# A split store, a new order of rotary units and pinned merge loads in a one-layer hybrid step

## The chip, the cores and the metric

The kernel runs on one core of a Trainium2 chip. The core has a matrix engine (TensorE, PE in the profile, with its weight loads shown as PEld), three engines for elementwise work (VectorE or DVE, ScalarE or ACT, GpSimd or POOL), and SyncE (SP), which here issues the transfers. The engines run their own instruction lists in order and meet by semaphores. The metric is the device time of one execution in microseconds. Each run comes with the granted clock of TensorE as a share of its full speed.

## The reference, cut to what matters

One layer of a hybrid backbone for 128 context and 1024 latent tokens, model width 1024. Both token groups go through the same weights, so the kernel carries them as one set of T = 1152 columns.

```python
def trunk_layer(x, mod, cache, lb, norm_g, ffn1, ffn2, mixer_w):
    m = [mod[:, i][:, None, :] for i in range(N_MOD)]
    x = x + 0.5 * m[2] * swiglu(modulate(x, norm_g[0], m[0], m[1]), *ffn1)
    mix, ctx = token_mixer(modulate(x, norm_g[1], m[3], m[4]), cache, lb, *mixer_w)
    x = x + m[5] * mix
    x = x + 0.5 * m[8] * swiglu(modulate(x, norm_g[2], m[6], m[7]), *ffn2)
    return x, ctx

# in token_mixer: attention of 8 heads and a two-way recurrent scan on the same input
    o_rec = rmsnorm(o_fw + flip(o_bw), hg_norm_g) * jax.nn.silu(heads(hgate, HG_DV))
    merged = jax.nn.sigmoid(ga) * (o_attn @ w_up_attn) + jax.nn.sigmoid(gr) * (o_rec @ w_up_rec)
    out = merged @ w_out
```

The keys of the attention have a rotary part that all heads share; its rotation depends on the position of a latent token on a grid. The results are the normalised x of both groups, the context's compressed keys, its rotary keys and its scan states.

## The kernel before

All values are float32. A product of two matrices is made of three matmuls: each operand is split into a high part, rounded by a cast to a shorter format, and a low part, the rest, and `mm3` (lines 516 to 518) adds high by high, high by low and low by high. So each operand costs a cast (as a rule on ScalarE) and a subtraction (on VectorE or GpSimd) before it can be used.

The stages follow one another on the columns: first feed-forward block, mixer, merge, second feed-forward block. In the mixer the recurrent part runs first. For each pair p of its heads, `proj_gate` ends with a gate: for each of three chunks of 384 columns, `put` multiplies the normalised scan output by the gate on GpSimd and stores the product, in full, in the DRAM tensor `orec`.

`attn` then makes the compressed keys, the rotary keys and the compressed queries. Units of 384 columns are run in a fixed list: k0, k1, k2 are the units of the compressed key (each has three steps: project and square, normalise, write) and r0, r1, r2 those of the rotary key (line 1276 on; a projection of 24 matmuls, then copies and products on VectorE that write tile `krt`). From the fifth step on, one step of `rec_half` is taken with each: it loads a quarter of the recurrent output, casts it on ScalarE and subtracts on VectorE (lines 1313 and 1314), since `rec_sums` computes the recurrent half of the merge's products for the two middle quarters of the columns in advance, and stores them in `ahead`.

`heads` runs eight heads, each in two blocks of 512 queries (`block`): scores against 9 key tiles, an exponential on ScalarE, its cast there (line 1512), its subtraction (line 1514) on VectorE or GpSimd, and the product with the values (`av`, lines 1481 to 1483), in which a block's output is divided by its sum (lines 1490 to 1493). In heads 6 and 7 a generator `preload` is stepped beside the blocks: it fetches what the merge will read, in chunks of 384 columns, and splits it (lines 1344 to 1346): four tiles of recurrent output, then three of attention output of heads 0 to 5. The last two heads' output is split as it comes, by `put_oat` (lines 1357 and 1358).

`merge` loads the eight x tiles and then runs `up(m)` for m = 0 to 7: the way-up weight of m is loaded, its attention half split on the chip (`raw`, `wh`, `wl`), and for each of four quarters of 288 columns the attention and the recurrent product (12 matmuls in each; the middle quarters take the recurrent one from `ahead` as tile `mu`) are multiplied by the gates `g` from `sgates`, added (tile `mt`) and split. That is 72 matmuls for each m. After m = 3, 5 and 7 a down-projection adds into x (line 545).

Tile framework and scheduler set the order: within an engine's list, instructions are placed by the scheduler's estimates unless they are pinned in program order. Transfers go out from SyncE's list one after another; a transfer that waits holds those behind it, and each one also waits until the one eight places before it has landed. Tiles of one tag share a number of buffers, so that a load waits for the last reader of an earlier tile.

Of the kernel before, what the change touches and what calls it, by code (L numbers as in the profile page):

```python
# [3 lines left out]

# [89 lines left out]
class Trunk:  # L94
# [594 lines left out]
    def mixer(self):  # L689
        nc, tc = self.nc, self.tc  # L690
        dram = lambda n, sh: self.dp.tile(sh, F32, name=n)
        self.sg = dram("sgates", [2, KT, P, T])
        self.orec = dram("orec", [4, P, T])
# [74 lines left out]
    def proj_gate(self, i, p, pair):  # L768
        nc = self.nc
        oT = pair["o"]  # L770
        assert pair["no"] == 4
        w = self.load_w(self.a["w_in"][i], KT, P, home="low")
        sq = self.tt(F32, "osq")[:, :T]
        nc.scalar.activation(sq, oT[:, :T], AF.Square)
        held, normed = [], []

        def norm():
            self.lnexp()
            for b in ORDER:
                self.rec_norm(b, oT, sq)  # L780
            normed.append(1)
            for f in held:
                f()

        def put(cs, s):
            nc.gpsimd.tensor_mul(s, oT[:, cs], s)
            nc.sync.dma_start(self.orec[p][:, cs], s)

        self.later.append(norm)
        for c in ORDER:  # L790
            ps = yield from self.proj_g(w, c)
            s = self.sigm(ps)
            nc.vector.tensor_mul(s, ps, s)  # L793
# [309 lines left out]
    def attn(self):  # L1103
# [10 lines left out]
        with tc.tile_pool(name="np", bufs=1, reuse_waits="tile") as self.fp:  # L1114
# [60 lines left out]
    def heads(self, qn, ck, ckc, KT_, ktc, rope, w0, sums):  # L1175
# [39 lines left out]
        for h in range(H):  # L1215
# [86 lines left out]
    def rec_half(self):  # L1302
# [3 lines left out]
        for k in range(4):  # L1306
            t = self.tt(F32R, "rec")
            self.rec.append((t[:, :n], t[:, n : 2 * n]))
            for v in range(2):
                c = ts(v, QW)  # L1310
# [25 lines left out]
    def preload(self):  # L1336
        nc = self.nc
        for k in (4, 5, 6, 7, 0, 1, 2):
            th, tl = self.mo[k] = self.tt(F32R, "oh"), self.tt(F32R, "ol")
            src = self.oat[k] if k < 4 else self.orec[k - 4]  # L1340
            for c in range(NCH):
                cs = slice(c * CW, (c + 1) * CW)
                raw = self.fp.tile([P, CW], F32, tag="vt", bufs=2, name="oraw")
                nc.sync.dma_start(raw, src[:, cs])
                (nc.vector.tensor_copy if k < 3 else nc.scalar.copy)(th[:, cs], raw)
                nc.vector.tensor_sub(tl[:, cs], raw, th[:, cs])
                yield

    def put_oat(self, h, r, cs, ob):
        nc = self.nc  # L1350
# [4 lines left out]
            self.mo[3] = self.tt(F32R, "oh"), self.tt(F32R, "ol")  # L1355
        th, tl = self.mo[3]
        nc.scalar.copy(th[r, cs], ob)
        nc.gpsimd.tensor_sub(tl[r, cs], ob, th[r, cs])

    def load_kv(self, src):  # L1360
        raw = self.wp.tile([P, 2, P], F32, tag="raw", bufs=2, name="raw")
# [193 lines left out]
    def merge(self):  # L1555
# [1 line left out]
        hl = self.mo  # L1557
        self.chunks, self.ticks = QORDER, 0
        self.x = []
        for k in range(KT):  # L1560
            t = self.tt(F32, f"x{k}")
            nc.sync.dma_start(t[:, :T], self.xs[k])
            self.x.append(t)

        def up(m):
            mh, ml = self.wide("mh", F32R), self.wide("ml", F32R)
            wh, wl = [self.wp.tile([P, KT, P], F32R, tag=t, bufs=3, name=t) for t in ("wh", "wl")]
            raw = self.wp.tile([P, 4, P], F32, tag="raw", bufs=2, name="raw")
            nc.sync.dma_start(raw, a["w_up"][m][:, :4])
            for i, w in enumerate((wh, wl)):  # L1570
                src = self.wrec[m // 2, i][:, 512 * (m % 2) : 512 * (m % 2) + 512]
                nc.sync.dma_start(w[:, 4:8].rearrange("p k m -> p (k m)").bitcast(F32), src)
            nc.scalar.copy(wh[:, :4], raw)
            nc.gpsimd.tensor_sub(wl[:, :4], raw, wh[:, :4])
            for c in QORDER:
                cs = slice(*c)
                mt = []
                for i in (1, 0):
                    g = self.slim("g")
                    nc.sync.dma_start(g, self.sg[i, m][:, cs])  # L1580
                    if i and REC[0] <= c[0] < REC[1]:
                        ps = self.fp.tile([P, QW], F32, tag="mu", bufs=4, name="mu")
                        nc.sync.dma_start(ps, self.ahead[m][:, c[0] - REC[0] : c[1] - REC[0]])
# [4 lines left out]
                    nc.vector.tensor_mul(t, ps, g)  # L1588
                    mt.append(t)
                nc.vector.tensor_add(mt[0], mt[1], mt[0])  # L1590
                nc.scalar.copy(mh[:, cs], mt[0])
# [751 lines left out]
```

## Time and profile before

| | |
|---|---|
| median of three runs | 2868.01 us (2866.91 to 2868.95) |
| the profiled execution | 2867.53 us, of which the span shown is 2865.3 us |
| granted TensorE clock over the span | 0.991 |
| TensorE busy | 2775.9 us, 97% |
| VectorE, ScalarE, GpSimd busy | 71%, 47%, 34% |
| rotary keys in the trace | about 1450 to 1470 us |
| heads 6 and 7 in the trace | about 1797 to 1878 us |
| merge in the trace | from 1878 us |

Rows of waits name the waiting engine, tile and line, then the engine, tile and line that released it, the total, the number of times and the longest wait. Rows of groups name line, engine, operation, written and read tiles, shapes and count, then busy time, mean ns of one, and the idle time before them with what ended it. A timeline row begins with the start and the duration. "128x288" is partitions by elements.

### The profile page before, as it was taken

The page shows a single profiled execution, that of the slowest core. Times are in us where ns is not written, and L with a number is a line of the kernel's source. Part 1 is how long each engine was busy: PE and PEld are TensorE (multiplying, and loading weights), DVE is VectorE, ACT ScalarE, POOL GpSimd, SP SyncE. Part 2 cuts the span into 40 slices and gives each one's busy share as a digit, 9 for nine tenths or more (in the row PEclk, how much of TensorE's full clock was granted, in tenths as well). Part 3 has the DMA queues.
Part 4 walks back from the last instruction along what each step waited for, and adds up shares of the span by engine and source line. Part 5 has one row for each costly group of instructions (what it writes and reads, how often), then busy time and mean ns, then how long its engine had stood idle before and what let it go on. Part 6 is the DMA issues. An engine that isn't in the chain of part 4 may idle for free. (4 is left out here: it accounts for less than half of the span.)

```text
span 2865.3 us, 55876 instructions
## 1 busy us (share of the span) xinstructions
PE 2775.9 (97%) x21222; PEld 2643.3 (92%) x21222; DVE 2029.3 (71%) x4439; ACT 1334.4 (47%) x2740; POOL 964.1 (34%) x1003
## 2 busy tenths in 40 slices
PE   8999999999999999999999999989989999999998
PEld 7999999999989999888998877789989999999997
DVE  7877777577678787876356677855765666558885
ACT  6522332321176677766535777731642322236332
POOL 0123232444222222222144444532442443424450
PEclk9999999999999999999999999999999999999999
DMA  6743443753122111112512001263543443447631
GB/s 260 228 133 119 126 127 111 250 178 118 58 70 68 43 60 38 55 46 68 181 43 77 16 16 30 82 215 99 177 154 115 144 156 119 129 143 213 202 101 67
DMA packets 218940, 331.76 MB, mean 116 GB/s; under 512 B 24048, under 2 KB 142768, under 8 KB 218672
## 3 DMA queue, kind: packets, MB, share of 16 engines
q1 hardware_dynamic: 218672, 328.20, 35.4%
q8 instruction: 167, 2.74, 0.4%
q14 instruction: 101, 0.83, 0.1%
HBM read 244.93 MB, written 83.18 MB: 115 GB/s over the span
## 5 line engine op out<-in xcount | busy, mean ns | idle before, releaser
L1802 PE MATMUL b<-xo,wo 128*128 128x288 f32 x3552 | 483.8, 295 | 1.1 <-DVE wo L1777 1.1
L1802 PEld LDWEIGHTS b<-xo,wo 128*128 128x128 f32 x3552 | 475.7, 188 | 1.3 <-DVE wo L1777 1.3
L1802 PE MATMUL b<-bh,wo 128*128 128x288 f32 x1776 | 368.0, 296 | 2.2 <-ACT et L1812 2.2
L516 PE MATMUL mm<-xh,wh 128*128 128x384 f32 x984 | 346.9, 353 | 14.1 <-DVE sg L793 5.8
L518 PE MATMUL mm<-xh,wl 128*128 128x384 f32 x984 | 335.0, 341 | 0.0
L517 PE MATMUL mm<-xl,wh 128*128 128x384 f32 x984 | 334.0, 339 | 0.0
L1802 PEld LDWEIGHTS b<-bh,wo 128*128 128x128 f32 x1776 | 290.4, 189 | 2.7 <-ACT et L1812 2.4
L545 DVE SCALAR_TENSOR_TENSOR x<-dn,modt,x 128x256 f32<-128x256 f32 (+4 forms) x472 | 225.5, 499 | 85.6 <-PE dn L518 83.7
L1802 PE MATMUL b<-bl,wo 128*128 128x288 f32 x888 | 262.5, 296 | 0.0
L1776 ACT CAST wo<-raw 128x512 fp32r<-128x512 f32 x185 | 114.7, 621 | 201.5 <-issue 85.7
L516 PEld LDWEIGHTS mm<-xh,wh 128*128 128x128 f32 x984 | 187.2, 190 | 23.0 <-DVE sg L793 7.7
L517 PEld LDWEIGHTS mm<-xl,wh 128*128 128x128 f32 x984 | 187.8, 191 | 1.1 <-issue 0.3
L2002 PE MATMUL d<-xd,wd 128*128 128x288 f32 x1344 | 179.9, 295 | 7.5 <-DVE x L1989 5.5
L518 PEld LDWEIGHTS mm<-xh,wl 128*128 128x128 f32 x984 | 187.1, 190 | 0.0
L2002 PEld LDWEIGHTS d<-xd,wd 128*128 128x128 f32 x1344 | 178.5, 188 | 8.9 <-DVE x L1989 2.7
L1777 DVE TENSOR_TENSOR wo<-raw,wo 128x512 fp32r<-128x512 f32 x185 | 127.4, 690 | 69.3 <-ACT wo L1776 66.7
L388 DVE SCALAR_TENSOR_TENSOR junk<-wada,cb 128x512 bf16<-128x512 f32 x224 | 162.1, 723 | 11.8 <-DMA wada<-in_w_aT 10.8
L1514 POOL TENSOR_TENSOR ehl<-e,ehl 128x512 fp32r<-128x512 f32 x93 | 122.1, 1318 | 140.4 <-ACT ehl L1512 73.6
L1802 PEld LDWEIGHTS b<-bl,wo 128*128 128x128 f32 x888 | 167.9, 189 | 0.0
L349 POOL TENSOR_TENSOR wl<-raw,wh 128x1024 fp32r<-128x1024 f32 (+2 forms) x48 | 95.7, 1995 | 161.2 <-ACT wh L348 121.0
L1777 DVE TENSOR_TENSOR wo<-ws,wo 128x512 fp32r<-128x512 f32 x74 | 71.4, 964 | 104.1 <-ACT wo L1776 103.6
L1776 ACT CAST wo<-ws 128x512 fp32r<-128x512 f32 x74 | 45.6, 618 | 211.9 <-POOL ws L1772 211.8
(456 smaller groups left out, 7223.1 us busy)
## 6 DMA issues: line engine op xcount, KB each, us to landing
raw<-in_w SPq DMA_DIRECT2D x148, 256.0 KB, 3.5
wada<-in_w_aT SPq DMA_DIRECT2D x112, 256.0 KB, 3.0
raw<-in_w SPq DMA_DIRECT2D x42, 512.0 KB, 3.9
raw<-in_w_in SPq DMA_DIRECT2D x41, 512.0 KB, 3.5
xr<-xd SPq DMA_DIRECT2D x56, 288.0 KB, 3.9
hr<-hs SPq DMA_DIRECT2D x26, 576.0 KB, 5.6
hb<-hd SPq DMA_DIRECT2D x44, 288.0 KB, 3.7
hs<-et SPq DMA_DIRECT2D x84, 144.0 KB, 2.2
```

Of the source, the lines that this page charges most:

```text
L349: pin((eng or self.nc.gpsimd).tensor_sub(wl, raw, wh))
L388: nc.vector.scalar_tensor_tensor(junk, ws[n % 2], 1.0, cs[s], ALU.mult, ALU.mult, accum_out=o)
L516: pin(nc.tensor.matmul(ps, wh, xh, start=start and i == 0, stop=False))
L517: pin(nc.tensor.matmul(ps, wh, xl, start=False, stop=False))
L518: pin(nc.tensor.matmul(ps, wl, xh, start=False, stop=stop and i == n - 1))
L545: nc.vector.scalar_tensor_tensor(self.x[m][:, a:b], ps[:, a - lo : b - lo], self.modt[:, gm, m, s : s + 1], self.x[m][:, a:b], ALU.mult, A ...
L1514: eng.tensor_sub(el, e, eh)
L1776: nc.scalar.copy(wh, src[i])
L1777: nc.vector.tensor_sub(wl, src[i], wh)
L1802: nc.tensor.matmul(ps, w[:, k], x[:, k, :QW], start=first, stop=last, skip_group_check=home != i)
L2002: nc.tensor.matmul(ps, w[:, k], xv, start=start, stop=stop, skip_group_check=home != i)
```

## The change

The recurrent output is stored split: `put` casts the product on ScalarE, subtracts on GpSimd, and stores the two parts with two transfers. Its readers, `rec_half` and `preload`, load both parts and compute nothing; `preload` loads them as whole tiles. The rotary units are spread over the list of units. For the last chunk of the compressed queries the subtraction is on VectorE. `preload` is stepped in all four blocks of heads 6 and 7, the cast and the subtraction of a chunk are two steps, and at its end it loads and splits the way-up weight of m = 0. The subtraction in `put_oat` goes to VectorE. In the merge the first m takes its quarters in the order 0, 3, 1, 2; the two gates of a part come in one transfer, four parts ahead, with `mu`; the x tiles are loaded two with each part; all these loads and those of the way-up weights are pinned in program order.

```diff
         def put(cs, s):
             nc.gpsimd.tensor_mul(s, oT[:, cs], s)
-            nc.sync.dma_start(self.orec[p][:, cs], s)
+            hi = self.fp.tile([P, CW], F32R, tag="t", bufs=3, name="ohi")
+            nc.scalar.copy(hi, s)
+            lo = s.bitcast(F32R)
+            nc.gpsimd.tensor_sub(lo, s, hi)
+            for v, t in enumerate((hi, lo)):
+                nc.sync.dma_start(self.orec[p, v][:, cs], t.bitcast(F32))
...
-                nc.gpsimd.tensor_sub(qn[i][1][:, cs], t, qn[i][0][:, cs])
+                eng = nc.vector if c == ORDER[-1] else nc.gpsimd
+                eng.tensor_sub(qn[i][1][:, cs], t, qn[i][0][:, cs])
...
-            for i, u in enumerate((k0, k1, k0, k2, k1, r0, r1, k2, r2)):
+            for i, u in enumerate((k0, r0, k1, k0, r1, k2, k1, r2, k2)):
...
-                    if not more and (h, j) != (6, 0):
+                    if not more:
                         next(pre, None)
...
-                raw = self.kp.tile([P, QW], F32, tag="gu", bufs=4, name="rraw")
-                nc.sync.dma_start(raw, self.orec[k][:, lo + v * QW : lo + (v + 1) * QW])
-                nc.scalar.copy(self.rec[k][0][:, c], raw)
-                nc.vector.tensor_sub(self.rec[k][1][:, c], raw, self.rec[k][0][:, c])
+                nc.sync.dma_start(self.rec[k][v].bitcast(F32), self.orec[k, v][:, lo:hi])
...
+            if k > 3:
+                for v, t in enumerate((th, tl)):
+                    nc.sync.dma_start(t[:, :T].bitcast(F32), self.orec[k - 4, v])
+                yield
+                continue
...
-                (nc.vector.tensor_copy if k < 3 else nc.scalar.copy)(th[:, cs], raw)
+                nc.sync.dma_start(raw, self.oat[k][:, cs])
+                nc.vector.tensor_copy(th[:, cs], raw)
+                yield
                 nc.vector.tensor_sub(tl[:, cs], raw, th[:, cs])
                 yield
+        self.up0 = self.load_up_all(0)
+        wh, wl, raw = self.up0
+        nc.scalar.copy(wh[:, :4], raw)
+        yield
+        nc.vector.tensor_sub(wl[:, :4], raw, wh[:, :4])
+        yield
+
+    def load_up_all(self, m):
+        nc, pin = self.nc, self.tc.keep_in_program_order
+        wh, wl = [self.wp.tile([P, KT, P], F32R, tag=t, bufs=3, name=t) for t in ("wh", "wl")]
+        raw = self.wp.tile([P, 4, P], F32, tag="raw", bufs=2, name="raw")
+        pin(nc.sync.dma_start(raw, self.a["w_up"][m][:, :4]))
+        for i, w in enumerate((wh, wl)):
+            src = self.wrec[m // 2, i][:, 512 * (m % 2) : 512 * (m % 2) + 512]
+            pin(nc.sync.dma_start(w[:, 4:8].rearrange("p k m -> p (k m)").bitcast(F32), src))
+        return wh, wl, raw
...
-        nc.gpsimd.tensor_sub(tl[r, cs], ob, th[r, cs])
+        nc.vector.tensor_sub(tl[r, cs], ob, th[r, cs])
...
+        first = [QUARTERS[q] for q in (0, 3, 1, 2)]
+        gates, parts = [], iter([(m, c) for m in range(KT) for c in (QORDER if m else first)])
+
+        def load_g(n=1):
+            for m, c in islice(parts, n):
+                g = self.half("g").rearrange("p (i n) -> p i n", i=2)
+                pin(nc.sync.dma_start(g, self.sg[:, m, :, slice(*c)].rearrange("i p n -> p i n")))
...
+                    pin(nc.sync.dma_start(mu, self.ahead[m][:, c[0] - REC[0] : c[1] - REC[0]]))
+                gates.append((g, mu))
+
+        def load_x(n):
+            for k in range(len(self.x), min(len(self.x) + n, KT)):
+                t = self.tt(F32, f"x{k}")
+                pin(nc.sync.dma_start(t[:, :T], self.xs[k]))
+                self.x.append(t)
...
+            if m:
+                wh, wl, raw = self.load_up_all(m)
+                nc.scalar.copy(wh[:, :4], raw)
+                nc.gpsimd.tensor_sub(wl[:, :4], raw, wh[:, :4])
+            else:
+                wh, wl, _ = self.up0
+                load_g(4)
+            for c in QORDER if m else first:
                 cs = slice(*c)
+                g, mu = gates.pop(0)
+                load_g()
+                load_x(2)
```

SyncE's list where attention ends and the merge begins, before the change (`oraw` are the preload's chunks, line 1562 loads x, 1580 the gates, 1583 `mu`; the way-up weights of m = 0 to 2, lines 1569 and 1572, stand some ten rows and more above this piece):

```order
L354 DMA raw<-in_w_out 128x1024
L1344 DMA oraw<-orec 128x384 x7
L1344 DMA oraw<-oat 128x384 x8
L1562 DMA x_21827<-xs 128x1152
L1344 DMA oraw<-oat 128x384
L1562 DMA x_21829<-xs 128x1152
L1562 DMA x_21831<-xs 128x1152
```

The x tiles go out between the last chunks of the preload. With the change (line 1366 and 1369 load a way-up weight, 1590 the gates, 1594 `mu`, 1600 x):

```order
L1369 DMA wh<-wrec 128x512
L1369 DMA wl<-wrec 128x512
L1590 DMA g<-sgates 128x2x288 [waits DVE_49,Pool_49]
L1590 DMA g<-sgates 128x2x288 [waits PE_49]
L1590 DMA g<-sgates 128x2x288
L1594 DMA mu<-ahead 128x288 [waits DMAHW4_49]
L1590 DMA g<-sgates 128x2x288 [waits DMAHW5_49]
L1594 DMA mu<-ahead 128x288 [waits DMAHW6_49]
L1590 DMA g<-sgates 128x2x288 [waits DMAHW7_49]
L1600 DMA x_21835<-xs 128x1152 [waits DMAHW0_49]
L1600 DMA x_21837<-xs 128x1152 [waits DMAHW1_49]
```

The weight above is that of m = 0. The second gate tile waits for TensorE, namely for the last matmul of the last head that reads the buffer in its place, and the x tiles come behind it. The same list further on, where the weight of m = 1 stands:

```order
L1600 DMA x_21913<-xs 128x1152 [waits DMAHW7_49]
L1600 DMA x_21915<-xs 128x1152 [waits DMAHW0_49]
L1590 DMA g<-sgates 128x2x288 [waits DMAHW1_49,DVE_49]
L1594 DMA mu<-ahead 128x288 [waits DMAHW2_49]
L1600 DMA x_21940<-xs 128x1152 [waits DMAHW3_49]
L1600 DMA x_21942<-xs 128x1152 [waits DMAHW4_49]
L1366 DMA raw<-in_w_up 128x512 [waits DMAHW5_49]
L1369 DMA wh<-wrec 128x512 [waits DMAHW6_49]
L1369 DMA wl<-wrec 128x512 [waits DMAHW7_49]
L1590 DMA g<-sgates 128x2x288 [waits DMAHW0_49,DVE_49]
```

It has moved from the blocks of attention to behind the last x tile.

VectorE's list at the first two rotary units, before the change (`krt`, `u`, `krf` and `ktc` belong to the rotary unit, `rt`, `nsq` and `nt` to the compressed key):

```order
L1295 TENSOR_TENSOR u<-u 32x256
L1290 COPY ktc_17080<-krt 32x128
L1290 COPY ktc_17081<-krt 32x128
L1290 COPY ktc_17082<-krt 32x128
L1290 COPY ktc_17083<-krt 32x128
L1283 COPY krt<-mm 64x384
L429 SCALAR_TENSOR_TENSOR rt<-nps,nsq 128x384
L1284 TENSOR_TENSOR krt<-krt,mm 64x384
```

and with the change:

```order
L1296 COPY ktc_17131<-krt 32x128
L1256 COPY nt<-mm 128x384 x2
L429 SCALAR_TENSOR_TENSOR rt<-nps,nsq 128x384
L430 SCALAR_TENSOR_TENSOR rt<-rt,nsq 128x384
L431 SCALAR_TENSOR_TENSOR nsq<-rt,nsq 128x384
L1289 COPY krt<-mm 64x384
L1267 SCALAR_TENSOR_TENSOR nt<-nt,vec,nsq 128x384 x2
L1140 COPY ckc<-nt 128x128 x2
L1290 TENSOR_TENSOR krt<-krt,mm 64x384
```

The second unit's read of its bank followed the first unit's last copy at once; a projection of the compressed key and its normalising now lie between them.

More of the change, by code (lines that the diff above doesn't have):

```diff
@@ L2 @@
 from functools import partial
-from itertools import chain
+from itertools import chain, islice
 import concourse.bass as bass
@@ L692, in mixer @@
         self.sg = dram("sgates", [2, KT, P, T])
-        self.orec = dram("orec", [4, P, T])
+        self.orec = dram("orec", [4, 2, P, T])
         self.oat = dram("oat", [4, P, T])
@@ L1339, in preload @@
             th, tl = self.mo[k] = self.tt(F32R, "oh"), self.tt(F32R, "ol")
-            src = self.oat[k] if k < 4 else self.orec[k - 4]
+            if k > 3:
[3 more added lines that the diff above has]
+                continue
             for c in range(NCH):
@@ L1559, in merge @@
         self.x = []
[L1560 to L1563, printed above, removed]
+        pin = self.tc.keep_in_program_order
+        first = [QUARTERS[q] for q in (0, 3, 1, 2)]
[4 more added lines that the diff above has]
+                pin(nc.sync.dma_start(g, self.sg[:, m, :, slice(*c)].rearrange("i p n -> p i n")))
+                mu = None
+                if REC[0] <= c[0] < REC[1]:
+                    mu = self.fp.tile([P, QW], F32, tag="mu", bufs=4, name="mu")
+                    pin(nc.sync.dma_start(mu, self.ahead[m][:, c[0] - REC[0] : c[1] - REC[0]]))
+                gates.append((g, mu))
@@ L1565, in up @@
+        def load_x(n):
[3 more added lines that the diff above has]
+                self.x.append(t)
         def up(m):
             mh, ml = self.wide("mh", F32R), self.wide("ml", F32R)
-            wh, wl = [self.wp.tile([P, KT, P], F32R, tag=t, bufs=3, name=t) for t in ("wh", "wl")]
-            raw = self.wp.tile([P, 4, P], F32, tag="raw", bufs=2, name="raw")
-            nc.sync.dma_start(raw, a["w_up"][m][:, :4])
@@ L1570, in up @@
[L1570 to L1575, printed above, removed]
+            if m:
[5 more added lines that the diff above has]
+                load_g(4)
@@ L1576, in up @@
+            for c in QORDER if m else first:
                 cs = slice(*c)
+                g, mu = gates.pop(0)
+                load_g()
+                load_x(2)
                 mt = []
                 for i in (1, 0):
[L1579 to L1583, printed above, removed]
+                    if i and mu:
+                        ps = mu
@@ L1587, in up @@
                     t = self.fp.tile([P, QW], F32, tag="hf", bufs=3, name="mt") if i else ps
-                    nc.vector.tensor_mul(t, ps, g)
+                    nc.vector.tensor_mul(t, ps, g[:, i])
                     mt.append(t)
```

2 lines of the change are left out of this document (removed).

## The prediction, on record before the run

> **What bounds the kernel now.** I read the page's totals first, then the list of waits of TensorE stretch by stretch, then windows with the granted clock, and last the DMA view and the timelines of SyncE and VectorE around the merge.
>
> ```profile
> span 2865.3 us, 55876 instructions
> PE 2775.9 (97%) x21222; PEld 2643.3 (92%) x21222; DVE 2029.3 (71%) x4439; ACT 1334.4 (47%) x2740; POOL 964.1 (34%) x1003
> ```
>
> TensorE is busy 97% of the span and the change takes no matmul away. So it can only win or lose what TensorE waits, and the half-speed clock that follows a wait. The waits that the diff can touch come from three answers of the list of waits (1340 to 1560, 1840 to 1880 and 1880 to 2130 us; columns: total us, times, longest):
>
> ```profile
> PE mm L516 <- DVE krt L1284: 3.6, 1, 3.6
> ...
> PE po L1483 <- DVE ehl L1514: 2.6, 1, 2.6
> PE mps L1464 <- DVE mx L1465: 1.4, 1, 1.4
> PE ptc L1534 <- DVE pc L1531: 0.7, 1, 0.7
> ...
> PE dn L516 <- DVE x L545: 4.8, 2, 2.5
> ...
> PE ups L516 <- ACT oh L1357: 1.4, 1, 1.4
> ...
> PE ups L516 <- DVE mt L1590: 1.1, 2, 0.9
> ...
> PE ups L517 <- POOL ol L1358: 1.0, 1, 1.0
> ```
>
> The windows around these waits (window, its length, busy TensorE and its instructions, granted clock, DMA share, GB/s) show a second price:
>
> ```profile
> 1465.00:1472.00 7.00, 5.37 (x17) 0.51 0.01 2
> ...
> 1868.00:1874.70 6.70, 6.43 (x16) 0.50 0.85 276
> ...
> 1885.00:1888.40 3.40, 3.40 (x17) 0.50 0.51 141
> 1923.00:1926.00 3.00, 0.68 (x7) 0.99 0.87 241
> 1926.00:1929.40 3.40, 3.40 (x14) 0.51 0.35 107
> 1972.00:1975.00 3.00, 0.57 (x5) 1.00 0.86 249
> 1975.00:1978.00 3.00, 2.97 (x22) 1.00 0.31 96
> ```
>
> Behind a wait the clock is granted at half for about 3.4 us, or twice that; a window of 3.4 us at half speed costs 1.7 us. Of the two equal waits at 1923 and 1972 us only the first is followed by it, so a short wait may or may not pay. The Trainium skill, "TensorE: Matmul & The Clock Gate", section "What's actually happening", has the gate fall only after an idle window of about 3.4 us that runs freely. The free phase agrees with the two rows above; the length does not, since a wait of 2.5 us was enough. By its length a wait of 2 to 3 us would cost no clock, which would leave out only the extra clock that I hold in the range below.
>
> **Gain A, rotary units.** In the row at L1284 TensorE's next bank waits for the second read of a rotary unit, which stands on VectorE behind the first two units, issued back to back. The new list k0, r0, k1, k0, r1, k2, k1, r2, k2 puts a projection of 3 to 6 us between them, and the last queries' subtraction goes from GpSimd to VectorE, which has no queue there. Removed: 3.6 us, and half of the 5.4 busy us at clock 0.51, 2.7: **6.3 us**. A shorter wait could stay at each of the three units, hence 3 to 6.3.
>
> **Gain B, heads 6 and 7.** Three windows of 40 us (columns: length, then busy PE, PEld, DVE, ACT, POOL, the clock, DMA share, GB/s), then VectorE in the last block:
>
> ```profile
> 1717.00:1757.00 40.00, 39.84 (x191) 32.09 (x190) 30.40 (x59) 31.35 (x62) 18.93 (x16) 1.00 0.06 14
> ...
> 1797.00:1837.00 40.00, 37.59 (x171) 28.70 (x169) 33.28 (x60) 31.47 (x63) 21.51 (x19) 1.00 0.29 85
> 1837.00:1877.00 40.00, 33.93 (x130) 23.70 (x128) 34.15 (x56) 28.54 (x54) 15.78 (x13) 0.91 0.43 128
> ```
>
> ```profile
> 1864.67 0.36 DVE L1345 CAST oh<-oraw 128x384 fp32r<-128x384 f32 x1 [1.13 <-DMA oraw<-oat]
> 1865.07 0.69 DVE L1493 SCALAR_TENSOR_TENSOR ob<-ob,rc 64x512 f32<-64x512 f32 x1
> 1865.79 0.56 DVE L1346 TENSOR_TENSOR ol<-oraw,oh 128x384 fp32r<-128x384 f32 x1
> 1866.26 0.16 DVE L1530 RECIPROCAL sums<-sums 128x1 f32<-128x1 f32 x1
> 1866.33 0.67 DVE L1514 TENSOR_TENSOR ehl<-e,ehl 128x512 fp32r<-128x512 f32 x1
> ```
>
> Against the quiet first window, TensorE idles 2.4 and 6.1 us in the last two, and the clock of 0.91 takes some 3.4 more: 11.9 us. The second view shows why: VectorE, in order, sits on a preload whose DMA is late, and the split of the exponentials that TensorE waits for (2.6 us) stands behind it. The change takes 12 casts (ScalarE) and 12 subtractions (VectorE) of the recurrent half out of this stretch, which arrives split, lets the preload begin a block earlier, and separates each cast from its subtraction; in the new order the last cast of the preload is issued before the last block. It adds the first way-up weight's cast and subtraction there, and one subtraction of a 64x512 piece per block on VectorE instead of GpSimd (some 0.7 us each, by the row of the same size at L1493). I take three quarters of the 11.9: **9.0 us**, with 3 if VectorE stays late and 12 if all goes.
>
> **Gain C, from attention to merge.** The first way-up bank now takes quarter 0, finished a block earlier, so the last head's piece is first needed at matmul 45 instead of 21. The cadence is between these rows, twenty steps in 2.64 us or 0.132 us each:
>
> ```profile
> 1877.99 0.29 PE L516 MATMUL ups<-oh,wh 128*128 128x288 f32 x1
> ...
> 1880.63 0.29 PE L518 MATMUL ups<-oh,wl 128*128 128x288 f32 x1
> ```
>
> That is 3.2 us of cover against waits of 1.4 and 1.0, and the half clock from 1885 (1.7) goes too: 4.1. VectorE must however finish the last head's output before its first gate product, which frees a bank; I leave 0.6 for that: **3.5 us**, 2 to 4.1.
>
> **Gain D, gates ahead of time.** This group of VectorE explains the two 2.5 us waits on L545 and those on L1590:
>
> ```profile
> L1588 DVE TENSOR_TENSOR mt<-mu,g 128x288 f32<-128x288 f32 x16 | 8.3, 521 | 25.4 <-DMA g<-sgates 25.1 <-issue 0.3
> ```
>
> VectorE waits 25.1 us for gates and then owes its products when the down-projection needs its reads. With gates four parts ahead these waits go: 4.8 + 1.1 + 1.7 of clock at 1926 = **7.6 us**, at least 5.
>
> **Loss E, the split store.** Twelve chunks get a cast on ScalarE and a subtraction on GpSimd, and 24 stores instead of 12. GpSimd's subtraction must precede the reuse of a gate tile, for which VectorE and then TensorE wait; the row of the page:
>
> ```profile
> L516 PE MATMUL mm<-xh,wh 128*128 128x384 f32 x984 | 346.9, 353 | 14.1 <-DVE sg L793 5.8
> ```
>
> TensorE already waits 5.8 us there, in four places. I charge **1.0 us**, 0 to 4 (a microsecond in each of the four).
>
> **Loss F, the second weight.** This is what speaks against the change. Before, the way-up weights of m = 1 and 2 were loaded inside attention, and the x tiles went out from 1866.74 on:
>
> ```profile
> 1866.74 0.42 SPq L1562 DMA_DIRECT2D x<-xs  x1
> ...
> 1870.08 6.41 SPq L1562 DMA_DIRECT2D x<-xs  x7
> ```
>
> Now all these loads are pinned in one order on SyncE. The second gate tile waits for the last attention matmul, call that T0, and everything behind it waits too: seven gate tiles of 288 KB, four mu of 144, eight x of 576, and then the three 256 KB transfers of m = 1. Sizes, median landing times, and rates (the two windows have all engines: PE, PEld, DVE, ACT, POOL, clock, DMA share, GB/s):
>
> ```profile
> g<-sgates SPq DMA_DIRECT2D x36, 144.0 KB, 3.3
> x<-xs SPq DMA_DIRECT2D x8, 576.0 KB, 7.3
> mu<-ahead SPq DMA_DIRECT2D x12, 144.0 KB, 3.2
> ...
> wh<-wrec SPq DMA_DIRECT2D x2, 256.0 KB, 3.7
> wl<-wrec SPq DMA_DIRECT2D x2, 256.0 KB, 4.9
> ```
>
> ```profile
> 1878.00:1882.00 4.00, 2.92 (x22) 2.69 (x20) 2.07 (x3) 1.58 (x3) 0.00 (x0) 1.00 1.01 410
> ...
> 1900.00:1910.00 10.00, 10.00 (x77) 10.00 (x76) 4.53 (x11) 2.25 (x5) 4.44 (x5) 1.00 0.87 249
> ```
>
> x (4.72 MB) at 410 GB/s takes 11.5 us; gates and mu (2.65 MB) at 249/0.87 = 286 GB/s, a stretch full of such 1152-byte rows, 9.3; the weights (0.79 MB) at about 300, 2.6. Together 23.4, so the weights are there at about T0 + 23.6. TensorE is done with m = 0 after 72 matmuls, 9.5 us, and the 0.6 left in C: it waits **13.5 us**. Bounds: all 8.16 MB at 410 gives 19.9 and a wait of 10; all at 249 gives 32.8 and 23. Behind so long a wait one slow window is sure: **1.7 us**. The Trainium skill, "DMA: Bandwidth & Descriptors", section "Bandwidth", gives 425 GB/s for a 16 MB load; by that an estimate of the transfer is 19.2 us and of the wait 9, which no row here supports for the 1152-byte part.
>
> **Loss G, the next two weights.** The transfers of m = 2 stand behind a gate tile whose buffer is freed by the second product of m = 1, some 7.2 us after that m starts (48 matmuls of 0.132 and a product and its sum, about 0.5 us each); with the issues ahead of them about 1.5 us and 3.7 of landing they come 12.4 us after it, against 9.5 needed: **3.0 us**. For m = 3 only the low half is so late, **2.0 us** (0 to 3 each way), without more clock, though 1.7 each is possible. From m = 4 on a down-projection of 192 matmuls, 25 us, hides the load.
>
> **Sum.** 6.3 + 9.0 + 3.5 + 7.6 = 26.4 gained; 1.0 + 13.5 + 1.7 + 3.0 + 2.0 = 21.2 lost; net 5.2 off the profiled run of 2867.53 (span 2865.3 and 2.2 around it). The median of the runs is 2868.01, half a microsecond more, so **2863 us**.
>
> **Rivals.** One: the second weight is not late, because the pinned loads start sooner or move faster than I reckon. For it: SyncE's queue has little else to issue. Against: the order has them behind the wait on attention's last matmul, and 10 us remain even at the best rate seen. Then F falls away (15.2 us) and with it most of G: 2868.0 - 26.4 + 1.0 + 2.0 = 2845. Two: the queue is slower, the other side. With all pinned transfers at 249 GB/s the wait before m = 1 is 23 us, each of the next two waits takes a slow window (3.4), and the head stretch gives only half (4.5): 21.9 gained, 33.1 plus 1.0 lost, 2868.0 + 12.2 = 2880. It is slower than before once the weights of m = 1 come later than T0 + 28.8, a rate under about 285 GB/s over the 8.16 MB. Three: the waits in attention don't go but move to another late piece (VectorE is busy 67 of 80 us in heads 6 and 7, and the split weight is added): A and B give 7.3 instead of 15.3, so 2868.0 - 18.4 + 21.2 = 2871. The rest does what it says.
>
> **Chances.** Forecast 0.50, rival one 0.20, two 0.10, three 0.20. The forecast's own range is 2855 to 2870 (F from 10 to 19, the others partly cancelling). A difference under 0.2%, 5.7 us, can't be told from none here. Faster by more takes a little under half of the forecast, 0.24, which lies on that bound, 0.03 of the third rival and all of the first: 0.47; slower takes the second and 0.07 of the third: 0.17; the rest, 0.36, is the same. For eight in ten I take 2849 to 2874, which leaves out the far parts of rivals one and two.
>
> **What would show it.** TensorE's list of waits should lose krt, the exponentials' row in the last block and both rows on x L545; a new row "ups waits for DMA wh" of 10 to 20 us should stand about 10 us after the last attention matmul, with a half-clock window behind it, and two of 2 to 3 us for the next weights. No such row means rival one. If krt or the last block still wait, A or B is wrong; if L793's row grows past 8 us, E is.

## The result and the profile after

| | before | with the change |
|---|---|---|
| median of 8 runs each | 2867.46 us (2859.17 to 2869.81) | 2876.14 us (2872.94 to 2878.59) |
| ratio, 95% interval | | 1.0034 (1.0026 to 1.0043) |
| profiled execution, its span | 2867.53, 2865.3 us | 2878.59, 2876.7 us |

The change makes the kernel 8.7 us slower (0.3%, clear of the noise), where 5.2 us less had been forecast. The page of the changed kernel:

```profile
span 2876.7 us, 55761 instructions
PE 2777.5 (97%) x21222; PEld 2647.1 (92%) x21222; DVE 2032.3 (71%) x4429; ACT 1333.5 (46%) x2732; POOL 965.1 (34%) x1005
```

TensorE's busy time rose by 1.6 us, and the span by 11.4. So nearly all of it is waiting. The table cuts both profiled executions at the first matmul of each stage (us; the scan's end is its last state matmul, the merge's its last down-projection):

| stage | before | after | difference | forecast |
|---|---|---|---|---|
| first feed-forward block | 826.5 | 824.4 | -2.1 | 0 |
| scan and gates | 558.6 | 563.6 | +5.0 | +1.0 (E) |
| last gate, keys and queries | 114.5 | 111.1 | -3.4 | -6.3 (A), with the next row |
| preparation of the heads | 52.0 | 49.8 | -2.2 | |
| heads 0 to 5 | 243.4 | 242.9 | -0.5 | 0 |
| heads 6 and 7 | 83.1 | 80.2 | -2.9 | -9.0 (B) |
| merge | 194.5 | 207.7 | +13.2 | +9.1 (C, D, F, G) |
| rest, second feed-forward block | 792.8 | 796.9 | +4.1 | 0 |

The two feed-forward blocks differ by +2.0 together, though nothing in them was changed. Over the 17 profiled executions of this study the first took from 822.9 to 827.0 us and the last stage from 791.5 to 796.9, so that differences of this size in them are not read as effects. Without them the stages give +9.2, close to the 8.7 of the medians. In the merge, the list of waits of TensorE (1880 to 1920, then 1920 to 2150 us):

```profile
PE ups L516 <- DMA wh<-wrec: 17.6, 2, 13.5
...
PE ups L518 <- POOL wl L1608: 1.0, 1, 1.0
PE ups L516 <- DMA wh<-wrec: 0.6, 1, 0.6
PE ups L518 <- DMA wl<-wrec: 0.4, 1, 0.4
```

The waits on x L545 are gone, and the way-up weights are waited for instead: 13.5 us before m = 1, 4.1 before m = 2, 2.0 in all at m = 3. The timeline of TensorE at the first, and of SyncE's queue ahead of it (start, duration):

```profile
1882.41 0.29 PE L518 MATMUL ups<-oh,wl 128*128 128x288 f32 x1
1896.18 0.58 PE L516 MATMUL ups<-oh,wh 128*128 128x288 f32 x1 [13.48 <-DMA wh<-wrec]
```

```profile
1871.79 1.40 SPq L1590 DMA_DIRECT2D g<-sgates  x3
...
1885.02 1.79 SPq L1600 DMA_DIRECT2D x<-xs  x2
1887.32 0.33 SPq L1366 DMA_DIRECT2D raw<-in_w_up  x1
1887.70 0.43 SPq L1369 DMA_DIRECT2D wh<-wrec  x1
```

The gate tiles leave at 1871.8, when attention's last matmul is done; the weight is issued 16 us later, behind all x tiles, and TensorE, finished with m = 0 at 1882.7, starts m = 1 at 1896.2, 24.4 us after T0 (23.6 had been reckoned). Windows of TensorE (length, busy, clock, DMA share, GB/s):

```profile
1882.50:1896.10 13.60, 0.20 (x2) 0.66 1.04 396
1896.50:1899.90 3.40, 3.40 (x15) 0.50 0.13 40
...
1912.30:1917.40 5.10, 5.10 (x22) 0.50 0.74 269
```

All sixteen transfer engines are full during the wait. The clock falls to half 4.1 us into the wait, which is why its mean there is 0.66, and stays so until 1900.4, for 4.2 us behind it. Behind the shorter wait before m = 2 the half clock lasts for 5.5 us, until 1917.5. In the rotary stage and in the heads (1340 to 1560, then 1800 to 1890 us):

```profile
PE mm L516 <- DVE sg L798: 1.5, 1, 1.5
PE nps L1262 <- POOL nsq L1259: 1.3, 1, 1.3
PE mm L516 <- ACT nsq L1257: 1.2, 1, 1.2
...
PE po L1506 <- POOL ehl L1537: 1.5, 3, 0.6
PE mps L1487 <- DVE mx L1488: 1.4, 3, 0.6
PE sps L1528 <- ACT qh L1495: 1.4, 1, 1.4
PE mtr L1494 <- DVE m L1491: 0.9, 2, 0.7
PE qps L516 <- DVE mx L1488: 0.8, 1, 0.8
PE ptc L1557 <- DVE pc L1554: 0.8, 1, 0.8
```

The rotary wait on `krt` is gone, with 1.3 and 1.2 us of others in its place. In heads 6 and 7 the single wait of 2.6 us is gone, but the list shows 6.8 us of small ones, spread over the blocks. Added up over just these two heads, the waits fell from 8.3 us (1797 to 1878 us, before) to 7.3 (1794 to 1872), and the stretches at half clock from 6.8 us to 3.4.

### The profile page after: what moved, and what is told of

Its sections match the earlier page's. It is cut to its first block, busy times and chain, and to the rows that moved or that the text cites. A ratio compares the mean times of both kernels' runs of the same rounds, so it can differ in the third digit from the quotient of the medians.

```text
span 2876.7 us, 55761 instructions
## 1 busy us (share of the span) xinstructions
PE 2777.5 (97%) x21222; PEld 2647.1 (92%) x21222; DVE 2032.3 (71%) x4429; ACT 1333.5 (46%) x2732; POOL 965.1 (34%) x1005
## 5 line engine op out<-in xcount | busy, mean ns | idle before, releaser
L545 DVE SCALAR_TENSOR_TENSOR x<-dn,modt,x 128x256 f32<-128x256 f32 (+4 forms) x472 | 225.9, 499 | 86.0 <-PE dn L518 84.5
L516 PE MATMUL ps<-bh,wh 128*128 128x288 f32 (+1 forms) x448 | 137.0, 306 | 7.3 <-DVE sl L1769 4.9
```

Source lines behind the costliest of these rows:

```text
L516: pin(nc.tensor.matmul(ps, wh, xh, start=start and i == 0, stop=False))
L545: nc.vector.scalar_tensor_tensor(self.x[m][:, a:b], ps[:, a - lo : b - lo], self.modt[:, gm, m, s : s + 1], self.x[m][:, a:b], ALU.mult, A ...
```

## The experiments

Times are medians with the ratio to the kernel before; the stage lengths are those of the table above. Line numbers of kernels that differ are their own.

**One: the weights of m = 1 and 2 early.** In the changed kernel, they are loaded behind that of m = 0 at the end of the preload.

```diff
+        self.ups += [self.load_up_all(m) for m in (1, 2)]
...
-                wh, wl, raw = self.load_up_all(m)
+                wh, wl, raw = self.ups[m] if m < 3 else self.load_up_all(m)
```

> The changed kernel with one thing different: the way-up weights of m = 1 and 2 are loaded right behind that of m = 0, at the end of the preload, ahead of the pinned gates and x tiles. Theory: the late weights are the largest loss of the change; the 13.6 us wait before m = 1 with its slow window (1.7) and the 4.3 us before m = 2 with its slow window (2.3) go, about 22 us, while m = 3 now has the full wait of some 3 us: 2876 becomes about 2856. Rival: the wait is one of bandwidth while eight x tiles move, and comes back at the next thing that is loaded (gates or the down-projection's x); then less than 8 us are won, 2868 or more.

Measured: 2847.7 us, 0.9946 (0.9934 to 0.9959), 28 us under the changed kernel by the medians, 25 by the two ratios. The merge takes 181.1 us instead of 207.7; every other stage is within 1.9 us. TensorE's waits from 1865 to 2130 us:

```profile
PE ps L516 <- DVE sl L1770: 3.3, 2, 2.2
PE ps L517 <- POOL bl L486: 2.2, 3, 1.4
PE ps L516 <- ACT bh L485: 0.7, 1, 0.7
PE ups L516 <- DVE mt L1626: 0.6, 1, 0.6
```

No wait for a weight is left, for m = 3 either, and none comes back at a gate or an x tile (the rows of `ps` belong to the second feed-forward block). So the late weights cost 26.6 us of the merge, and without them the merge is 13.4 us shorter than before the change. The 0.6 at the first gate product is the one that the prediction left over in C.

**Two: the split store alone**, in the kernel before, with the readers that load both parts.

```diff
+            nc.scalar.copy(hi, s)
+            nc.gpsimd.tensor_sub(lo, s, hi)
+            for v, t in enumerate((hi, lo)):
+                nc.sync.dma_start(self.orec[p, v][:, cs], t.bitcast(F32))
...
```

> The kernel before with the split store alone and the readers that load both parts; no other part of the change. Theory: the cast on ScalarE waits there, in order, for GpSimd's product, and what is queued behind it reaches TensorE late, so the scan stage grows by about 5 us (558.6 to 563 or 564); some 2 to 3 come back where the readers save casts and subtractions: 2869 to 2871. Rival: the 5 us of the scan in the changed kernel are a difference of waits and slow windows from one execution to another; the scan stays within 1 us of 558.6 and the time is 2864 to 2867.

Measured: 2870.3 us, 1.0019 (1.0011 to 1.0028). The scan takes 563.2 us, 4.6 more than before, the keys 1.1 less and heads 6 and 7 3.5 less. The time and the scan are as expected; whether for the reason given, the cast on ScalarE, this run does not show. Two things follow. The loss in the scan belongs to this part of the change; and heads 6 and 7 gain as much by it alone (79.6) as by the whole change (80.2). The waits in the scan (824 to 1390 us), before:

```profile
PE mm L516 <- DVE sg L793: 4.1, 3, 1.8
PE mm L516 <- DVE q L738: 3.9, 3, 1.9
PE vt L756 <- ACT t L749: 2.9, 3, 1.6
PE lv L1003 <- DVE QP L1040: 1.4, 1, 1.4
```

and in the changed kernel:

```profile
PE mm L516 <- DVE sg L798: 7.2, 5, 1.8
PE mm L516 <- DVE q L738: 5.0, 4, 2.3
...
PE vt L756 <- ACT t L749: 3.3, 4, 1.6
PE lv L1008 <- DVE QP L1045: 3.0, 3, 1.9
PE dS L1070 <- ACT kT L1062: 1.2, 1, 1.2
```

Each row grew a little, the gate tile's and the scan's own (`lv`, `dS`) alike.

**Three: the cast of the split store on GpSimd**, in the changed kernel.

```diff
-            nc.scalar.copy(hi, s)
+            nc.gpsimd.tensor_copy(hi, s)
```

> The changed kernel with the cast of the split store on GpSimd, between the product and the subtraction that are there anyway, instead of on ScalarE. Theory (ScalarE's list is blocked by the cast): the scan stage loses most of its 5 us, 563.6 to 559 or 560, and the time goes from 2876 to about 2872. Rival (GpSimd's longer work per chunk is what delays the gate tiles and the scan's own GpSimd steps): the scan grows further, to 565 or more, and the time to 2877 or more.

Measured: 2877.6 us, 1.0047 (1.0034 to 1.0059), scan 563.8. Taking the cast off ScalarE gave nothing; it did not grow to 565 either. So the cast's place on ScalarE's list is not the main cause of the loss.

**Four: the rotary order alone**, in the kernel before.

```diff
-            for i, u in enumerate((k0, k1, k0, k2, k1, r0, r1, k2, r2)):
+            for i, u in enumerate((k0, r0, k1, k0, r1, k2, k1, r2, k2)):
```

> The kernel before with the new list of rotary and key units alone. Theory: the 3.6 us wait on the rotary tile and its 2.7 us of slow clock go and nothing comes in their place, stage 1406 to 1552 us shorter by 5 to 6.3, time 2861 to 2862.5. Rival: the wait goes to other units of the list (the key's normalising now starts later), and no more than 3 us are won, 2864.5 or more.

Measured: 2860.8 us, 0.9985 (0.9976 to 0.9994). Keys take 109.5 instead of 114.5 us, preparation 51.8 instead of 52.0: 5.2 less. The waits from 1390 to 1500 us:

```profile
PE mm L516 <- DVE sg L793: 1.4, 1, 1.4
PE nps L1256 <- POOL nsq L1253: 1.3, 1, 1.3
```

The key's normalising is late by 1.3 us in place of the 3.6 of `krt`, and no slow window is left. This part does what it was taken to do.

**Five to eight** start from the kernel of the first experiment (2847.7 us). Five steps the preload on two of every three key tiles, six puts the subtraction of the last heads' output on GpSimd again, seven the subtraction of the split store on VectorE, eight its product on VectorE.

```diff
# five
-                    if not more:
+                    if not more and t % 3 < 2:
# six
-        nc.vector.tensor_sub(tl[r, cs], ob, th[r, cs])
+        nc.gpsimd.tensor_sub(tl[r, cs], ob, th[r, cs])
# seven
-            nc.gpsimd.tensor_sub(lo, s, hi)
+            nc.vector.tensor_sub(lo, s, hi)
# eight
-            nc.gpsimd.tensor_mul(s, oT[:, cs], s)
+            nc.vector.tensor_mul(s, oT[:, cs], s)
```

> The kernel with the early weights (first experiment, 2847.7 us), with the preload stepped on two of every three key tiles of heads 6 and 7, so that its 24 steps end in the last block instead of in the one before. Theory: what is left of waits there (8.7 us against a quiet stretch) comes from VectorE being full where the preload now runs (19.1 of 20 us in the second block); spread out, heads 6 and 7 lose 2 to 4 us of their 80, 2844 to 2846. Rival: the waits are set by the order of the row maxima and the splits of the exponentials, not by the preload; no more than 1 us, or a wait for the first weight at the merge: 2847 to 2850.

Measured: 2844.5 us, 0.9919 (0.9907 to 0.9932); heads 6 and 7 74.7 us instead of 79.9.

> The kernel with the early weights, with the low part of the last heads' output subtracted on GpSimd as before instead of on VectorE. Theory: VectorE is the full engine in heads 6 and 7, so this part of the change is worth nothing or less there; heads 6 and 7 are 0 to 1.5 us shorter, and the end of attention, where GpSimd needs 1.3 us instead of 0.7, costs up to 1: 2846.5 to 2848.5. Rival: the part helps as it was charged; the time is 2849 or more.

Measured: 2845.4 us, 0.9928 (0.9916 to 0.9941); heads 6 and 7 78.5 us, the merge 0.8 less. In this kernel the subtraction on VectorE was worth less than nothing in that stage, as expected.

> The kernel with the early weights, with the subtraction of the split store on VectorE instead of GpSimd; the cast stays on ScalarE. Theory one (GpSimd's twelve subtractions lengthen VectorE's own work and delay the scan's steps): the scan stage goes from 563 to 560 or 561, time about 2845. Theory two (ScalarE, in order, waits for GpSimd's product before the cast): nothing changes in that wait, the scan stays at 562.5 or more, and VectorE may now wait too: 2847 to 2850.

Measured: 2847.2 us, 0.9933 (0.9919 to 0.9946); scan 562.9.

> The kernel with the early weights, with the product of the split store on VectorE instead of GpSimd; cast on ScalarE and subtraction on GpSimd stay. GpSimd then has as many operations per chunk as before the change, and ScalarE's cast no longer waits for a 1.3 us product behind GpSimd's other work. Both theories of the last experiment: the scan stage goes from 563 to 559 or 560, time 2843 to 2845. Rival: VectorE, 71% busy, pays for the product itself: the scan stays at 562 or more, 2847 or more.

Measured: 2846.1 us, 0.9927 (0.9915 to 0.9939); scan 562.0, one microsecond less and not four. Whichever engine had which operation, the scan stayed at 562 to 564.

**Nine to twelve.** Eleven joins five and six; nine is eleven with the split of a chunk put off to the end of the next group of scan steps; ten is eleven with the store whole, split by the readers, and the preload (now 32 steps) on all key tiles; twelve is ten with the last subtraction on VectorE. "The third run here" in the expectations is eleven.

```diff
# nine
+            self.later.append(partial(split, cs, s))
# ten
+            nc.sync.dma_start(self.orec[p][:, cs], s)
...
+                nc.scalar.copy(self.rec[k][0][:, c], raw)
+                nc.vector.tensor_sub(self.rec[k][1][:, c], raw, self.rec[k][0][:, c])
```

> The kernel with the early weights, the spread preload and the last split on GpSimd together. The three stand at different places, so their gains add: 2847.7 less 3 to 5 (heads 6 and 7) less 1.5 to 2: 2841 to 2843, heads 6 and 7 at 73 to 75 us. Rival: the two in heads 6 and 7 remove the same wait, 2844.5 or more.

Measured: 2849.5 us, 0.9927 (0.9914 to 0.9939); heads 6 and 7 80.6 us. By the ratios, it can't be told from five (0.9919) and six (0.9928). The two gains did not add, and in its profiled execution, the slowest of its five, the stage shows neither, which the expectation had not foreseen. The waits there with five alone (1788 to 1880 us), then with both (1780 to 1890 us):

```profile
PE ptc L1558 <- DVE pc L1555: 1.5, 2, 0.8
PE mps L1488 <- DVE mx L1489: 1.1, 2, 0.7
...
PE po L1507 <- POOL ehl L1538: 0.6, 2, 0.4
```

```profile
PE mps L1488 <- DVE mx L1489: 2.8, 3, 1.8
PE po L1507 <- POOL ehl L1538: 2.6, 2, 1.3
PE po L1505 <- ACT ehl L1536: 1.5, 1, 1.5
```

Row maxima and exponentials' splits are among the late pieces in both, in different shares.

> The kernel of the third run here (early weights, spread preload, last split on GpSimd), with the cast, subtraction and stores of a recurrent chunk put off to the end of the next group of scan steps, so that they stand behind other work in the lists. Theory (ScalarE, in order, waits at the cast for the product, and the scan's copies queue behind it): the cast comes when its product is done, the scan stage goes from 563 to 559 or 560, about 3.5 us under the third run. Rival (it is the added work on ScalarE, GpSimd and the queue, wherever it stands): the scan stays at 562.5 or more, within 1 us of the third run.

Measured: 2846.0 us, 0.9923 (0.9909 to 0.9936); scan 562.9. Putting the split elsewhere gives nothing.

> The kernel of the third run here, with the recurrent output stored whole as before the change and split by its readers (ScalarE casts, VectorE subtracts), the preload on all key tiles of heads 6 and 7. Theory (the split store alone costs the scan 4.6 to 5 us): the scan is back at 558 to 559; the rotary and key stage loses 1, heads 6 and 7 lose up to 3.5 of their 75: 0 to 3.5 us under the third run, about 2840. Rival: the readers' work costs as much as the scan gains, the time is that of the third run or more.

Measured: 2839.4 us, 0.9900 (0.9887 to 0.9914), the fastest of the study, 28.7 us under the kernel before, run beside it. The scan takes 557.9 us, 5.4 under eleven; keys 1.0 less, and heads 6 and 7 79.9, no more than with the split store. These stages give 7.1 us, where 0 to 3.5 had been expected. The medians differ by 10.1; 2.9 us between the two profiled executions lies in the feed-forward blocks, where nothing was changed.

> The kernel that stores the recurrent output whole (2839.4 us), with the last heads' low part subtracted on VectorE, as in the spread-preload run that had heads 6 and 7 at 74.7 us. Theory: with the preload spread over four blocks, VectorE has room and GpSimd's 1.3 us subtraction is the late piece; heads 6 and 7 go from 79.9 to about 75, time 2835. Rival: that stage depends on which piece of VectorE's list stands in front of which split, and not on either part by itself; 78 us or more, 2838 or more.

Measured: 2845.5 us, 0.9924 (0.9910 to 0.9937); heads 6 and 7 80.9 us. The rival holds: what had gone with 74.7 us in five brings nothing here.

**Thirteen to fifteen** take the split store apart, in the kernel of eleven. They leave out part of the computation: thirteen stores the product twice, fourteen stores the high part and the whole product, fifteen subtracts the scan output from the product, on GpSimd, and stores that twice.

```diff
# thirteen
+            for v in range(2):
+                nc.sync.dma_start(self.orec[p, v][:, cs], s)
# fourteen
+            nc.scalar.copy(hi, s)
+            for v, t in enumerate((hi.bitcast(F32), s)):
# fifteen
+            nc.gpsimd.tensor_sub(s, s, oT[:, cs])
```

> The kernel with early weights, spread preload and the last split on GpSimd, but the recurrent product is stored twice as it is, without cast and subtraction (the low part that the readers get is therefore not the rest but the product). Theory (the operations cost the scan its 5 us, not the stores): scan stage at 558 to 559. Rival (the second transfer on SyncE's queue, or the gate tile held until it has read): 562 or more.

Measured (one run): 2843.7 us, scan 558.1.

> The same with the cast on ScalarE and two stores, without the subtraction on GpSimd (the second store is the whole product). If ScalarE's in-order wait at the cast is the cause: scan stage at 562 or more. If GpSimd's subtraction is: 558 to 559.5. If both share it: about 560 to 561.

Measured (one run): 2842.6 us, scan 559.3.

> The same with a subtraction on GpSimd and two stores, without the cast (the subtraction takes the scan output instead, so the stored values are not the split). If GpSimd's subtraction is the cause: scan stage at 562 or more. If ScalarE's wait at the cast is: 558 to 559.5. If both share it: about 560 to 561.

Measured (one run): 2846.4 us, scan 563.7.

With the store whole, unsplit, the scan took 557.9 to 558.6 us in four kernels. So the second store costs it nothing; against thirteen, the cast on ScalarE costs 1.2 us, and GpSimd's subtraction alone 5.6, the whole of the loss. Why, is seen in VectorE's timeline in a gate phase, beside GpSimd's. With stores only:

```profile
1187.28 0.56 DVE L431 SCALAR_TENSOR_TENSOR osq<-rt,osq 128x384 f32<-128x384 f32 x1
...
1187.92 0.61 DVE L1102 SCALAR_TENSOR_TENSOR oT<-oT,vec,osq 128x384 f32<-128x384 f32 x1
...
1193.62 1.97 DVE L1041 TENSOR_TENSOR QP<-QP,T 64x192 f32<-64x192 f32 x2
```

With the subtraction:

```profile
1186.61 1.27 DVE L431 SCALAR_TENSOR_TENSOR osq<-rt,osq 128x384 f32<-128x384 f32 x1
...
1187.97 1.19 DVE L1103 SCALAR_TENSOR_TENSOR oT<-oT,vec,osq 128x384 f32<-128x384 f32 x1
...
1194.25 2.95 DVE L1042 TENSOR_TENSOR QP<-QP,T 64x192 f32<-64x192 f32 x2
...
1186.33 1.14 POOL L786 TENSOR_TENSOR sg<-oT,sg 128x384 f32<-128x384 f32 x1
1187.55 1.20 POOL L787 TENSOR_TENSOR sg<-sg,oT 128x384 f32<-128x384 f32 x1
...
1193.75 1.34 POOL L787 TENSOR_TENSOR sg<-sg,oT 128x384 f32<-128x384 f32 x1
```

The same VectorE operation takes 1.27 instead of 0.56 us, 1.19 instead of 0.61 and 2.95 (two operations) instead of 1.97 where it begins while a GpSimd operation is running. The first two end 0.4 us after that GpSimd operation does (1187.88 behind 1187.47, 1189.16 behind 1188.75), as if they had waited for it. These operations are the recurrent norm and the scan's own steps, which TensorE waits for. Matched operation by operation between thirteen and fifteen, VectorE falls behind in each of the three gate phases of the scan, by 2.5, 2.3 and 2.4 us (1063 to 1073, 1187 to 1196 and 1321 to 1331 us of thirteen), and in all three it is longer operations that make the loss, not later starts. A part is caught up behind the last of them, where VectorE had waited for TensorE anyway; 5.6 us are left. The Trainium skill, "Perfetto Trace Analysis", section "Optimizing Scalar/DVE Operations", has GpSimd and VectorE share a read port of the on-chip memory, so that moving work between them might not help; these rows agree with that, though they show the lengthening and not the port. It also fits that seven, with the subtraction on VectorE, gained nothing: by the same matching VectorE falls behind there by 1.4, 1.9 and 1.4 us in the three phases, in each by about the time of its own three subtractions (0.56 us each).

## Why the prediction was wrong, step by step

**A, rotary units** (6.3): 5.6 measured in the two stages, 5.2 with this part alone. Right, and the 1.3 us wait at the key's norm is the kind of leftover that was allowed for.

**B, heads 6 and 7** (9.0): 2.9. This step failed. It took the casts and subtractions of the preload for the cause, because one late transfer stood ahead of the 2.6 us wait, and took three quarters of all lost time as the share. Experiment two gets 3.5 of it from the split store alone, and ten gives the split store back without losing them. With the preload spread, unspread, on more or fewer tiles, and the last split on either engine, the stage took 78.5 to 80.9 us in every variant of the changed kernel but one, which had 74.7. What is shown is that TensorE's waits there did not go but moved: 8.3 us before, 7.3 with the change, now for row maxima, exponentials' splits and other short pieces; most of the rest of the 2.9 is the half clock, 3.4 us of it instead of 6.8. That the order of short operations in VectorE's and GpSimd's lists decides is the reading that fits, and is not shown by itself. What would hold the stage at 74.7 stays open.

**C and D, transition and gates** (11.1): 13.4, by experiment one. Right, and a little small; the slow windows behind the waits went with them.

**E, the split store** (1.0, up to 4): 5.0. The term was mis-sized and its mechanism was wrong. It looked for GpSimd's subtraction in the way of a gate tile and priced the four waits at that tile. What the runs show is that the subtraction lengthens VectorE's operations beside it, in the recurrent norm and in the scan, so that the price is paid at `lv`, `dS` and `q` too. A hint stood in the trace of before, in the preload in heads 6 and 7, in the durations (min, median, max in ns) of one VectorE operation of one shape, which the prediction did not ask about, and in the rows beside it:

```profile
L1346 DVE TENSOR_TENSOR ol<-oraw,oh x21: 542/559/1653, 1799.9 to 1875.8; 128x384 fp32r<-128x384 f32 x21
...
1858.72 1.62 DVE L1346 TENSOR_TENSOR ol<-oraw,oh 128x384 fp32r<-128x384 f32 x1
...
1858.65 1.28 POOL L1514 TENSOR_TENSOR ehl<-e,ehl 128x512 fp32r<-128x512 f32 x1 [4.29 <-ACT ehl L1512]
```

Of the 21, seven took 0.74 to 1.65 us and the others 0.54 to 0.56. Each of the seven began while a GpSimd operation was running, and ended 0.4 us after it, here at 1860.35 behind 1859.93. Those that began ahead of the GpSimd operation were not lengthened by it.

**F, the second weight** (13.5 and 1.7 of clock): 13.5, and 4.2 us at half clock, 2.1 by the prediction's own reckoning of half the stretch. Right in place, mechanism and size, and it was the largest single term. The weight was there 24.4 us after T0, where 23.6 had been reckoned. The rates that were put in for x (410 GB/s) and for gates (286) are not confirmed one by one: in the wait the mix moved at 396.

**G, the next weights** (5.0, no clock): 4.1 before m = 2 and 2.0 at m = 3, a wait for a split among them, and behind them 5.5 and 3.0 busy us at half clock, 2.7 and 1.5 by the same reckoning. So the size of this term failed: the clock, which the prediction called possible and left out of the sum, was paid at both. F and G together cost 26.6 by experiment one, instead of 20.2; the waits and the half clock named here add up to 25.9.

So the sum missed by 14.4: 6.1 in B, 4.0 in E, 6.4 in F and G, 0.7 in A, less 2.3 in C and D and 0.5 in heads 0 to 5. Only C and D and heads 0 to 5 went for the change, and every other term against it; the range had let them cancel. Rival three (the attention's waits move to another late piece) is what happened in B, and its 2871 with the 4.0 more of E comes to 2875, about what was measured. That is in part luck, since the 6.4 more of F and G and the 2.3 less of C and D are in neither. Rival one did not happen in the change, and experiment one shows about what it would have been: 2847.7, where 2845 had been worked out, with a larger B and a smaller E than were measured.

## What to carry to other kernels

When loads are pinned in program order on one queue, write down for each late tile how many bytes stand before it and when the first of them may start: here a 256 KB weight stood behind some 7.4 MB that could not start before the last matmul of the stage, and loading it and the next one earlier was worth 25 to 28 us. GpSimd is only 34% busy, but work given to it is not free while VectorE works on the critical chain: look for one VectorE operation with two durations in the trace and see what runs beside the longer one. And where a stage is limited by the order of short operations on a full engine, a gain reckoned from removed work should be given with its lower end, since here edits that helped alone did not add.

## What the runs showed of the hardware that was not expected

Subtractions of 128x384 on GpSimd, 1.0 to 1.3 us each and nine of the twelve inside the scan stage, made VectorE's operations beside them 2.3 times as long (0.56 to 1.27 us) and the scan 5.6 us longer, while the second stores of 192 KB cost it nothing and the casts on ScalarE 1.2 us. In the rows above, a VectorE operation that began while GpSimd's was running ended 0.4 us after it.

The stretches at half clock begin on a grid of 3.41 us within each of the 17 profiled executions. Taken over all of them from 170 us on, a step of this grid at full clock was always followed by half clock when TensorE had been busy for less than 45% of it, and never when for more than 68%; in between both occur. This bears on the two equal waits before the change that the prediction could not tell apart: the one that ended at 1926 us lay within one step, in which TensorE was busy for 34%, and the one that ended at 1975 us was cut in two by a border, with 66% and 62% busy.
